# The small operations of a norm move from SBUF into the PSUM bank of its sums

## The chip, the cores and the metric

The kernel runs on one core of a Trainium2 chip. The metric is the device time of one execution in microseconds (us): before the change 1384.69, the median of three runs (1383.99 to 1385.03). A core has five engines with their own instruction queues: TensorE (PE in the profile; its weight loads are PEld), VectorE (DVE), ScalarE (ACT), GpSimd (POOL) and SyncE (SP), from whose queue most DMAs are issued. SBUF and PSUM are its memories; TensorE writes PSUM, in 8 banks of 512 fp32 numbers per partition.

## What is computed

Two layers of a decoder, on 1024 tokens of width 1024 in fp32. Each layer normalises its input, modulates it with vectors made from c, projects it, runs two kinds of attention (layer 0: latent and windowed; layer 1: differential and forgetting), gates the result, projects it back, normalises again and adds it to x. Every norm has this form:

```python
def rmsnorm(x, g):
    xf = x.astype(jnp.float32)
    y = xf * lax.rsqrt(jnp.mean(xf * xf, axis=-1, keepdims=True) + NORM_EPS)
    return (y * g.astype(jnp.float32)).astype(x.dtype)

for layer in range(DEPTH):
    mod = cond @ w_ada[layer] + b_ada[layer]
    shift, scale, gate = jnp.split(mod, 3, axis=-1)
    h = rmsnorm(x, g_pre[layer]) * (1.0 + scale[:, None, :]) + shift[:, None, :]
    y = even_mixer(h, ...) if layer % 2 == 0 else odd_mixer(h, ...)
    x = x + gate[:, None, :] * rmsnorm(y, g_post[layer])
```

The latent attention also normalises its two low-rank inputs, and the differential attention each head's output.

## The kernel before

Tiles are 128 channels by 512 tokens (C = 512), so the tokens form two halves, ch or c 0 and 1. An fp32 product is made of three matmuls: weights and activations are split into a high and a low part (split, L89 to L92: ScalarE writes the high part, VectorE or GpSimd the low one), and kstep (L124) issues high by high (L127), high by low (L128) and low by high (L130). A projection accumulates 8 such steps in a PSUM bank named pj, S or o. PSUM is given out by tag: S one tile of two banks, pt two banks, pj two, o two.

**The norm.** Channels lie on partitions, so the mean over channels is a sum over partitions, and TensorE makes it. rstd (L197) takes the squares s, summed over channel tiles, and multiplies them with a column of ones (L204): four matmuls leave the sum of each token in a pt bank, 128 tokens by 4 columns. VectorE turns it into the inverse root by eleven operations on 128x4 numbers. L206 makes the variance v from the bank; L207 makes a first guess y from v's bits; then three Newton rounds: w = -0.5 v y (L209), w = w y (L210), y = (w + 1.5) y (L212). v, w and y are small SBUF tiles of the tag sm, which has 24 buffers. Then TensorE broadcasts y over the partitions into another pt bank (L216): each column of y, stretched to 128x128, times the identity, so four matmuls. The bank r is what rstd returns, and the caller multiplies by it. Each fp32 matmul shows in the profile as two rows, so the four are x8 there.

rstd runs 21 times: twice for the input of layer 0 (run), four times for the low-rank inputs (keep, in even_first; two of them write the last y into the constant rkc), twice for the input of layer 1 (to_odd), five times for the outputs of the layers (residual), and 8 times for the heads of the differential attention (diff_items).

**What sets the order.** Each engine works through its queue in order. A scheduler in the framework builds the queues from the program, by its own estimate of what each instruction costs, and adds the waits. The program itself interleaves: project() with the norms around it, weave() with attention and projections, and ada_behind() spreads the product of c with w_ada through the projections: VectorE accumulates loaded tiles of in_wadab into the tile ad (L282), ScalarE starts each sum (L285).

Other lines that the steps touch: the softmax of a block is L463 on VectorE (row minimum from S) and L465 on ScalarE (exp with row sums); L941 and L942 in diff_items make the factor of the second map from these sums, L944 combines the two maps; L474 and L475 make reciprocal row sums for a layout change; L356 is the gate; L673 the low part of a low-rank input; L678 its squares added on GpSimd; L549 and L553 finish a head; L687 the rotation of the shared key; L246 casts a mask.

Of the kernel before, what the change touches and what calls it, by code (L numbers as in the profile page):

```python
# [33 lines left out]
class Trunk:  # L34
# [162 lines left out]
    def rstd(self, s, n, col=None):  # L197


        nc = self.nc  # L200
        nb = s.shape[-1] // 128
        p = self.psum("pt")
        for b in range(nb):
            nc.tensor.matmul(p[:, b:b + 1], s[:, b * 128:b * 128 + 128], self.ones, start=True, stop=True)  # L204
        v, w, y = (self.small(nb) for _ in range(3))
        nc.vector.tensor_scalar(v, p[:, :nb], 1.0 / n, EPS, op0=ALU.mult, op1=ALU.add)  # L206
        nc.vector.tensor_scalar(y.bitcast(I32), v.bitcast(I32), -0.5, 1597463007.0, op0=ALU.mult, op1=ALU.add)  # L207
        for i in range(3):
            nc.vector.scalar_tensor_tensor(out=w, in0=v, scalar=-0.5, in1=y, op0=ALU.mult, op1=ALU.mult)  # L209
            nc.vector.tensor_tensor(out=w, in0=w, in1=y, op=ALU.mult)  # L210
            z = col if i == 2 and col is not None else y
            nc.vector.scalar_tensor_tensor(out=z, in0=w, scalar=1.5, in1=y, op0=ALU.add, op1=ALU.mult)  # L212
        y = z
        r = self.psum("pt")[:, :nb * 128]
        for b in range(nb):
            nc.tensor.matmul(r[:, b * 128:b * 128 + 128], y[:, b:b + 1].to_broadcast([128, 128]), self.ident,  # L216
                             start=True, stop=True)
        return r
# [1218 lines left out]
```

## Time and profile before

| | us |
|---|---|
| median of 3 runs | 1384.69 |
| the profiled execution | 1385.66 |
| its span in the trace | 1383.9 |
| PE busy | 1281.1 (93%) |
| DVE busy | 918.0 (66%) |
| ACT busy | 731.9 (53%) |
| POOL busy | 334.2 (24%) |

The 1.8 us between the profiled execution and its span lie outside the trace. A row of the timeline gives start and length in us, engine, line, operation, the tile written and the tiles read (buffer numbers left out), their shapes, and in brackets how long the engine had stood idle before and what it waited for. A row of waits gives who waited for whom: us in total, times, and the longest. A group of a line gives busy us and the mean ns of one, then the idle time before; the rows of one source line give the shortest, median and longest ns. In a table of stretches each row has start and end, their length, the busy us of PE, PEld, DVE, ACT and POOL with their counts, the clock that TensorE was granted (1.00 is full speed), the DMA share and GB/s.

### The profile page before, as it was taken

The numbers are of one execution on the slowest core, as the hardware profiler recorded it, in microseconds if no ns is written. First come the engines' busy times: TensorE is split into PE (matmuls) and PEld (weight loads), VectorE is DVE, ScalarE is ACT, GpSimd is POOL, SyncE is SP. The second block draws the span as 40 slices with busy tenths as digits, with TensorE's granted clock in tenths as the row PEclk, the third lists the DMA queues.
The fourth block names the chain that finished last, engine by engine and source line by source line (L and its number), as shares of the span: only waits on it lengthen the run. The fifth ranks groups of instructions, "written<-read, shape, count | busy, mean of one in ns | idle before, by whom it ended". The sixth has DMA issues, their size and how long they took to land.

```text
span 1383.9 us, 20791 instructions
## 1 busy us (share of the span) xinstructions
PE 1281.1 (93%) x6940; PEld 1060.0 (77%) x6940; DVE 918.0 (66%) x1963; ACT 731.9 (53%) x1507; POOL 334.2 (24%) x316
## 2 busy tenths in 40 slices
PE   2798999999999999899989999999999999999996
PEld 2577788888777777777767778787888888888896
DVE  6855666777668775787977785767645464655375
ACT  4252126665557577764545544446445454556552
POOL 2242422331233215300013232221212111112400
PEclk9899999999999999999999999999999999999998
DMA  8605586556354544373633222212112121233283
GB/s 291 236 19 168 169 286 221 164 168 178 97 172 132 158 132 131 108 232 110 193 89 94 75 70 68 57 49 88 58 46 75 49 85 54 84 107 107 77 262 127
DMA packets 105132, 175.98 MB, mean 127 GB/s; under 512 B 16688, under 2 KB 25904, under 8 KB 105024
## 3 DMA queue, kind: packets, MB, share of 16 engines
q1 hardware_dynamic: 100512, 172.03, 39.4%
q10 hardware_dynamic: 4512, 2.62, 0.6%
q8 instruction: 54, 0.88, 0.3%
q14 instruction: 54, 0.44, 0.1%
HBM read 131.45 MB, written 31.74 MB: 118 GB/s over the span
## 4 chain that ended last, share of the span: by engine, by line
PE 59%; DVE 21%; issue 7%; ACT 6%; DMA 5%; POOL 1%; SPq 1%; DVEq 0%; POOLq 0%; ACTq 0%
PE pj L127 10%; PE pj L128 10%; PE pj L130 9%; PE S L441 7%; PE pt L500 4%; PE o L510 2%; DVE p L463 2%; PE S L127 2%; PE S L130 2%; PE o L509 2%; PE S L128 2%; DVE pt_l L92 2%; PE pt L216 1%; DVE acc L282 1%; DMA wr<-in_wout_dram 1%
## 5 line engine op out<-in xcount | busy, mean ns | idle before, releaser
L127 PE MATMUL pj<-h,wh 128*128 128x512 f32 (+1 forms) x816 | 340.6, 418 | 1.0 <-ACT wh L91 1.0
L128 PE MATMUL pj<-h,wh 128*128 128x512 f32 (+1 forms) x816 | 321.6, 394 | 0.0
L130 PE MATMUL pj<-h,wl 128*128 128x512 f32 (+1 forms) x800 | 314.9, 394 | 2.7 <-DVE wl L92 2.7
L92 POOL TENSOR_TENSOR wl<-wr,wh 128x512 fp32r<-128x512 f32 x126 | 164.2, 1311 | 462.7 <-ACT wh L91 424.4
L465 ACT ACTIVATE p<-p,sm 128x128 f32<-128x128 f32 (+3 forms) x192 | 148.7, 775 | 148.0 <-DVE sm L463 143.5
L92 DVE TENSOR_TENSOR pt_l<-pt,pt_h 128x512 fp32r<-128x512 f32 (+1 forms) x232 | 147.1, 635 | 107.4 <-ACT pt_h L91 105.7
L441 PE MATMUL S<-qk,qk 96*128 96x512 f32 (+5 forms) x720 | 174.6, 344 | 20.4 <-DVE sm L463 10.9
L91 ACT ACTIVATE pt_h<-pt 128x512 fp32r<-128x512 f32 (+1 forms) x232 | 127.8, 552 | 96.1 <-PE pt L500 92.5
L130 PEld LDWEIGHTS pj<-h,wl 128*128 128x128 f32 x800 | 150.5, 188 | 34.5 <-DVE wl L92 3.6
L441 PEld LDWEIGHTS S<-qk,qk 128*128 128x128 f32 (+1 forms) x720 | 120.8, 189 | 62.6 <-DVE sm L463 26.2
L127 PEld LDWEIGHTS pj<-h,wh 128*128 128x128 f32 (+1 forms) x816 | 153.6, 188 | 19.0 <-ACT wh L91 1.9
L128 PEld LDWEIGHTS pj<-h,wh 128*128 128x128 f32 (+1 forms) x816 | 154.1, 189 | 16.3 <-DVE h L92 0.2
L91 ACT ACTIVATE wh<-wr 128x512 fp32r<-128x512 f32 x165 | 101.2, 622 | 111.2 <-PE S L128 40.8
L500 PE MATMUL pt<-ident,p 128*128 128x128 f32 x840 | 134.4, 274 | 2.6 <-DVE p L944 2.6
L500 PEld LDWEIGHTS pt<-ident,p 128*128 128x128 f32 x840 | 101.2, 140 | 25.6 <-DVE p L944 4.1
L463 DVE CUSTOM_DVE_ANT_0 p<-S,mask 128x640 f32<-128x640 f32 (+7 forms) x128 | 95.9, 749 | 32.7 <-PE S L441 32.1
L509 PE MATMUL o<-pt_h,v 128*128 128x256 f32 (+1 forms) x408 | 106.5, 281 | 1.3 <-ACT pt_h L91 0.8
L510 PE MATMUL o<-pt_l,v 128*128 128x256 f32 (+1 forms) x408 | 102.3, 285 | 4.9 <-DVE pt_l L92 4.7
L347 POOL TENSOR_TENSOR t<-t,rs 128x512 f32<-128x512 f32 x26 | 36.8, 1417 | 230.8 <-DMA t<-t 208.3
L510 PEld LDWEIGHTS o<-pt_l,v 128*128 128x128 f32 x408 | 77.2, 189 | 14.8 <-DVE pt_l L92 9.6
L509 PEld LDWEIGHTS o<-pt_h,v 128*128 128x128 f32 x408 | 77.1, 189 | 9.5 <-ACT pt_h L91 3.4
L463 DVE CUSTOM_DVE_ANT_0 p<-S,x 128x128 f32<-128x128 f32 (+3 forms) x64 | 48.2, 753 | 25.0 <-PE S L445 21.8
(315 smaller groups left out, 2311.3 us busy)
## 6 DMA issues: line engine op xcount, KB each, us to landing
wr<-in_wod_dram SPq DMA_DIRECT2D x80, 256.0 KB
wr<-in_wout_dram SPq DMA_DIRECT2D x68, 256.0 KB
ad<-in_wadab_dram SPq DMA_DIRECT2D x41, 256.0 KB
wr<-in_wev_dram SPq DMA_DIRECT2D x38, 256.0 KB
raw<-in_wadaa_dram SPq DMA_DIRECT2D x32, 256.0 KB
ogd<-t SPq DMA_DIRECT2D x32, 256.0 KB
t<-t SPq DMA_DIRECT2D x106, 64.0 KB
t<-rd SPq DMA_DIRECT2D x48, 128.0 KB
```

What stands on the lines that cost most here:

```text
L91: nc.scalar.activation(hi, src, AF.Copy)
L92: (lo_eng or nc.vector).tensor_tensor(out=lo, in0=src, in1=hi.bitcast(F32), op=ALU.subtract)
L127: nc.tensor.matmul(p, w[0][:, k, :m], h[0], start=first, stop=False)
L128: nc.tensor.matmul(p, w[0][:, k, :m], h[1], start=False, stop=last and w[1] is None)
L130: nc.tensor.matmul(p, w[1][:, k, :m], h[0], start=False, stop=last)
L347: nc.gpsimd.tensor_tensor(out=s, in0=s, in1=self.rs[:, cs], op=ALU.mult)
L441: nc.tensor.matmul(dst, a, k[:, s], start=(n == 0), stop=(n == len(q) - 1 and not more))
L463: nc.vector.tensor_tensor_reduce(out=P[:, :n], in0=S[:, :n], in1=add, scale=-scale, scalar=init, op0=ALU.add, op1=ALU.min, accum_out=nm)
L465: nc.scalar.activation(P[:, :n], P[:, :n], AF.Exp, bias=nm, scale=-1.0, accum_out=l)
L500: nc.tensor.transpose(pt[:, n * 128:n * 128 + 128], b, self.ident)
L509: nc.tensor.matmul(o[:, qcols], w, hi[:, cols], start=start, stop=False)
L510: nc.tensor.matmul(o[:, qcols], w, lo[:, cols], start=False, stop=stop)
```

## The change

```diff
     def rstd(self, s, n, col=None):
 
 
+
         nc = self.nc
         nb = s.shape[-1] // 128
         p = self.psum("pt")
         for b in range(nb):
             nc.tensor.matmul(p[:, b:b + 1], s[:, b * 128:b * 128 + 128], self.ones, start=True, stop=True)
-        v, w, y = (self.small(nb) for _ in range(3))
+        v, w, y = p[:, 8:8 + nb], p[:, 16:16 + nb], self.small(nb)
         nc.vector.tensor_scalar(v, p[:, :nb], 1.0 / n, EPS, op0=ALU.mult, op1=ALU.add)
```

v and w become columns 8 and 16 on of p, the pt bank that holds the sums. y stays in SBUF. So L206 goes from PSUM to PSUM, L207 from PSUM to SBUF, L209 and L210 read one operand in PSUM and y in SBUF and write PSUM, L212 reads w in PSUM and y in SBUF and writes SBUF. Before, all but L206 had all operands in SBUF. Each norm takes one sm buffer instead of three, and p stays in use until the last L212. The counts of instructions stay: 231 of these small operations. A blank line moves all lines from 200 on up by one, so L206 of before is L207 of after.

The scheduler also orders the queues differently. Three places:

**TensorE at the third norm** (the first low-rank input of the first half; S_969 and S_957 are the bank of a projection that runs meanwhile, pt_828 and pt_822 the broadcast of this norm, pt_835 and pt_829 the sums of the next). Before:

```order
L127 MATMUL S_969<-h_316,wh_944 128x512
L128 MATMUL S_969<-h_317,wh_944 128x512
L130 MATMUL S_969<-h_316,wl_945 128x512
L216 MATMUL pt_828<-ident,sm_816 128x128 x4
L204 MATMUL pt_835<-ones,t_641 128x1 x4
L127 MATMUL S_969<-h_396,wh_944 128x512
```

After, from the same matmul on:

```order
L127 MATMUL S_957<-h_314,wh_932 128x512
L128 MATMUL S_957<-h_315,wh_932 128x512
L130 MATMUL S_957<-h_314,wl_933 128x512
L127 MATMUL S_957<-h_394,wh_932 128x512
L128 MATMUL S_957<-h_395,wh_932 128x512
L130 MATMUL S_957<-h_394,wl_933 128x512
L127 MATMUL S_957<-h_399,wh_932 128x512
L217 MATMUL pt_822<-ident,sm_810 128x128 x4
L205 MATMUL pt_829<-ones,t_637 128x1 x4
L128 MATMUL S_957<-h_400,wh_932 128x512
```

The broadcast moved behind four more matmuls of the projection; between it and its own sums stand 16 matmuls, where 12 stood.

**VectorE at the same norm**, from the second small operation on (sm_814, sm_815, sm_816 are v, w, y before; pt_805 holds v and w after). Before:

```order
L207 TENSOR_SCALAR sm_816<-sm_814 128x4
L209 SCALAR_TENSOR_TENSOR sm_815<-sm_814,sm_816 128x4
L210 TENSOR_TENSOR sm_815<-sm_815,sm_816 128x4
L212 SCALAR_TENSOR_TENSOR sm_816<-sm_815,sm_816 128x4
L209 SCALAR_TENSOR_TENSOR sm_815<-sm_814,sm_816 128x4
L210 TENSOR_TENSOR sm_815<-sm_815,sm_816 128x4
L673 SCALAR_TENSOR_TENSOR qk_803<-pj_777,vecs,qk_802 128x512
L212 SCALAR_TENSOR_TENSOR sm_816<-sm_815,sm_816 128x4
L209 SCALAR_TENSOR_TENSOR sm_815<-sm_814,sm_816 128x4
L210 TENSOR_TENSOR sm_815<-sm_815,sm_816 128x4
L212 SCALAR_TENSOR_TENSOR sm_816<-sm_815,sm_816 128x4
L246 CAST mask<-t_913 128x128
```

After:

```order
L208 TENSOR_SCALAR sm_810<-pt_805 128x4
L210 SCALAR_TENSOR_TENSOR pt_805<-pt_805,sm_810 128x4
L211 TENSOR_TENSOR pt_805<-pt_805,sm_810 128x4
L213 SCALAR_TENSOR_TENSOR sm_810<-pt_805,sm_810 128x4
L674 SCALAR_TENSOR_TENSOR qk_799<-pj_773,vecs,qk_798 128x512
L210 SCALAR_TENSOR_TENSOR pt_805<-pt_805,sm_810 128x4
L211 TENSOR_TENSOR pt_805<-pt_805,sm_810 128x4
L213 SCALAR_TENSOR_TENSOR sm_810<-pt_805,sm_810 128x4
L210 SCALAR_TENSOR_TENSOR pt_805<-pt_805,sm_810 128x4
L211 TENSOR_TENSOR pt_805<-pt_805,sm_810 128x4
L247 CAST mask<-t_901 128x128
L213 SCALAR_TENSOR_TENSOR sm_810<-pt_805,sm_810 128x4
```

The low part of the low-rank input (L673) stands one round earlier, and the cast of the mask moved ahead of the norm's last operation.

**VectorE at the end of the first head norm of the differential attention** (sm_7923 and sm_7901 are its y; the reciprocal works on the row sums of the softmax block that runs meanwhile). Before:

```order
L209 SCALAR_TENSOR_TENSOR sm_7922<-sm_7921,sm_7923 128x4
L210 TENSOR_TENSOR sm_7922<-sm_7922,sm_7923 128x4
L212 SCALAR_TENSOR_TENSOR sm_7923<-sm_7922,sm_7923 128x4
L941 RECIPROCAL sm_7964<-sm_7964 128x1
L942 SCALAR_TENSOR_TENSOR sm_7964<-sm_7964,nlam,sm_7691 128x1
```

After:

```order
L210 SCALAR_TENSOR_TENSOR pt_7896<-pt_7896,sm_7901 128x4
L942 RECIPROCAL sm_7942<-sm_7942 128x1
L211 TENSOR_TENSOR pt_7896<-pt_7896,sm_7901 128x4
L943 SCALAR_TENSOR_TENSOR sm_7942<-sm_7942,nlam,sm_7671 128x1
L213 SCALAR_TENSOR_TENSOR sm_7901<-pt_7896,sm_7901 128x4
```

The last two operations of the norm moved behind the reciprocal. On SyncE's queue, in the same part of the program as the third to sixth norm, two loads of in_wl moved ahead of loads of in_wadab.

## The prediction

> **What bounds the kernel now.** I read the page first, then PE's waits, then the timeline around the longest of them.
>
> ```profile
> span 1383.9 us, 20791 instructions
> PE 1281.1 (93%) x6940; PEld 1060.0 (77%) x6940; DVE 918.0 (66%) x1963; ACT 731.9 (53%) x1507; POOL 334.2 (24%) x316
> PE 59%; DVE 21%; issue 7%; ACT 6%; DMA 5%; POOL 1%; SPq 1%; DVEq 0%; POOLq 0%; ACTq 0%
> ```
>
> TensorE (PE) is busy for 93% and carries most of the chain that ended last. VectorE (DVE) carries a fifth of it. So the small operations matter only where PE stands still for them, and PE's waits for the broadcast (L216) say how much that is:
>
> ```profile
> PE pt L216 <- DVE sm L212: 9.7, 6, 3.4
> PE pt L216 <- issue: 2.3, 1, 2.3
> PE pt L216 <- DVE rkc L212: 1.1, 1, 1.1
> ```
>
> That is 13.1 us over 8 of the 21 norms. The last norm shows what the chain of eleven small operations costs with nothing else in the way (start, length, both in us):
>
> ```profile
> 1372.81 0.16 DVE L206 TENSOR_SCALAR sm<-pt 128x2 f32<-128x2 f32 x1 [0.76 <-PE pt L204]
> ...
> 1374.77 0.16 DVE L212 SCALAR_TENSOR_TENSOR sm<-sm,sm 128x2 f32<-128x2 f32 x1
> 1375.08 0.68 PE L216 MATMUL pt<-ident,sm 128*128 128x128 f32 x4 [2.31 <-DVE sm L212]
> ```
>
> Ten steps take 1374.77 - 1372.81 = 1.96 us, 0.196 each, and PE resumes 2.27 us after L206 started. The first norm's 2.3 us ("issue") is of the same kind. The longest wait is not:
>
> ```profile
> 111.03 1.30 POOL L678 TENSOR_TENSOR t<-t,t 128x512 f32<-128x512 f32 x1 [5.20 <-ACT t L671]
> 111.27 1.08 DVE L207 TENSOR_SCALAR sm<-sm 128x4 int32<-128x4 int32 x1
> 112.28 3.20 POOL L92 TENSOR_TENSOR p<-wr,p 128x512 fp32r<-128x512 f32 x3
> 112.38 1.21 DVE L209 SCALAR_TENSOR_TENSOR sm<-sm,sm 128x4 f32<-128x4 f32 x1
> 113.62 1.19 DVE L210 TENSOR_TENSOR sm<-sm,sm 128x4 f32<-128x4 f32 x1
> 114.85 0.65 DVE L212 SCALAR_TENSOR_TENSOR sm<-sm,sm 128x4 f32<-128x4 f32 x1
> 115.81 0.75 DVE L673 SCALAR_TENSOR_TENSOR qk<-pj,vecs,qk 128x512 fp32r<-128x512 f32 x1
> 117.36 2.05 PE L216 MATMUL pt<-ident,sm 128*128 128x128 f32 x8 [3.43 <-DVE sm L212]
> ```
>
> Four operations on four numbers per partition take 1.08, 1.21, 1.19 and 0.65 us. L207 ends at 112.35, as GpSimd's (POOL) 111.03 instruction ends at 112.33; L212 ends at 115.50, as POOL's three end at 115.48. They are held while POOL runs, and go on when it changes instruction or stops. Which instructions are held?
>
> ```profile
> L206 DVE TENSOR_SCALAR sm<-pt x21: 150/161/163, 22.0 to 1372.8; 128x4 f32<-128x4 f32 x19, 128x2 f32<-128x2 f32 x2
> L209 DVE SCALAR_TENSOR_TENSOR sm<-sm,sm x63: 143/162/1205, 22.4 to 1374.4; 128x4 f32<-128x4 f32 x57, 128x2 f32<-128x2 f32 x6
> L549 DVE TENSOR_TENSOR t<-o,t x48: 641/689/696, 232.4 to 1314.6; 64x512 f32<-64x512 f32 x48
> L553 DVE TENSOR_TENSOR t<-t,g x24: 679/684/1749, 266.0 to 1316.0; 128x512 f32<-128x512 f32 x24
> ```
>
> The numbers are shortest, median and longest in ns. L553, with both inputs in SBUF, is stretched to 1749 ns; L549, one of whose inputs is the PSUM tile o, never passes 696 in 48. L206 reads PSUM alone and stays at 163, while L209 goes to 1205. An operation that takes an input from PSUM was not held; L207, held above, takes its only input from SBUF.
>
> **The change part by part.** *The operands.* All eleven operations of a norm now take their first tensor input from the bank. So the holding should end for them. What it costs in all:
>
> ```profile
> L207 DVE TENSOR_SCALAR sm<-sm 128x4 int32<-128x4 int32 (+1 forms) x21 | 5.4, 258 | 0.5
> L209 DVE SCALAR_TENSOR_TENSOR sm<-sm,sm 128x4 f32<-128x4 f32 (+1 forms) x63 | 11.2, 177 | 1.7
> L210 DVE TENSOR_TENSOR sm<-sm,sm 128x4 f32<-128x4 f32 (+1 forms) x63 | 13.5, 214 | 1.6
> L212 DVE SCALAR_TENSOR_TENSOR sm<-sm,sm 128x4 f32<-128x4 f32 (+1 forms) x61 | 12.6, 207 | 1.8
> ```
>
> 42.7 us for 208 instructions; at 0.16 each it would be 33.3, so 9.4 us of VectorE's time is holding. Only what reaches PE counts.
>
> *The duration.* L206 reads PSUM in 161 ns, L209 reads SBUF in 162, so reading costs nothing. No VectorE row writes PSUM, so I bound that: not below -0.02 us per operation (L209's shortest against its median), not above +0.16 (the operation doubled). I take 0, because the nearest row, L206, shows no price for PSUM on its reading side. [...]
>
> *The order.* The scheduler places the broadcast later on PE, as the first rows shown with the change tell of the norm that made PE wait at 117.36. Four matmuls moved ahead of the broadcast: 16 stand between it and its sums, where 12 stood. A matmul of this form takes 0.23 us, start to start:
>
> ```profile
> 130.99 0.40 PE L127 MATMUL S<-h,wh 128*128 128x512 f32 x1
> 131.22 0.40 PE L128 MATMUL S<-h,wh 128*128 128x512 f32 x1
> ```
>
> Elsewhere the same happens, by 2 to 10 matmuls or scores, except in the first and last norm and in that of the second to_odd, where the distance stays. On VectorE (the second rows shown with the change) one cast came in ahead of the norm's last operation. Unheld, the chain is 2.27 us, plus 0.55 for L674 (before's L673: 0.75 long, in place of a 0.2 step) and 0.2 for the cast: about 3.0 us, from 111.1 to 114.1. PE ran dry at 117.36 - 3.43 = 113.93; with four matmuls more it reaches the broadcast at 114.86. The wait goes entirely. What is late next there is PE itself.
>
> *The clock.* A wait of that length costs twice (stretch, length, PE busy and count, then the other engines, then granted clock):
>
> ```profile
> 117.40:123.80 6.40, 6.40 (x23) 5.82 (x24) 3.28 (x15) 0.80 (x2) 0.00 (x0) 0.50 0.13 41
> 123.80:129.00 5.20, 5.20 (x25) 4.21 (x25) 3.93 (x11) 0.60 (x1) 0.00 (x0) 1.00 0.82 269
> 810.10:813.10 3.00, 2.99 (x12) 2.79 (x13) 1.73 (x4) 0.90 (x2) 0.04 (x1) 0.50 0.00 0
> ```
>
> For 6.4 us behind the wait the granted clock is 0.50: 3.2 us lost. Behind the wait at 810.11 it is 0.50 for 3.0 us: 1.5 lost. The three other waits that can go, with what held the chain at two of them:
>
> ```profile
> 135.45 1.15 DVE L210 TENSOR_TENSOR sm<-sm,sm 128x4 f32<-128x4 f32 x1
> 138.13 1.13 PE L216 MATMUL pt<-ident,rkc 128*128 128x128 f32 x8 [1.15 <-DVE rkc L212]
> 776.44 0.82 PE L216 MATMUL pt<-ident,sm 128*128 128x128 f32 x5 [1.15 <-DVE sm L212]
> 806.08 1.22 DVE L212 SCALAR_TENSOR_TENSOR sm<-sm,sm 128x4 f32<-128x4 f32 x1
> 808.13 1.11 DVE L210 TENSOR_TENSOR sm<-sm,sm 128x4 f32<-128x4 f32 x1
> 810.11 2.08 PE L216 MATMUL pt<-ident,sm 128*128 128x128 f32 x8 [2.25 <-DVE sm L212]
> ```
>
> At 138.13, 1.0 us of holding goes and six matmuls (1.4 us) more stand ahead: 1.15 gained. At 810.11 the rows at 806.08 and 808.13 alone hold 1.06 and 0.95 us: 2.0 of the 2.25 from these, the rest from the matmul and the two scores that now stand ahead; 2.25 gained. At 776.44 a new wait comes. As the third rows shown with the change tell, the norm's last two operations now stand behind the reciprocal of the next softmax block (L941, now L942):
>
> ```profile
> DVE sm L941 <- ACT p L465: 14.8, 20, 1.4
> ```
>
> The reciprocal waits for row sums from ScalarE (14.8 / 20, 0.7 us a time), and behind it wait the two operations, the broadcast on PE and all that PE has behind that. I count 0.2 of the 1.15 as gained there. Elsewhere the reciprocal of L474 comes in the same way; the 2 to 10 matmuls ahead of the broadcast cover it.
>
> *The bank.* p is held until the chain's end, not until L206. The next use of that bank stands behind the broadcast on PE in all 21 norms, so it costs nothing; without that cover it would cost a chain, 2 us. Two of 24 buffers fewer per norm cost nothing: no wait is for them.
>
> *The sum.* 3.4 + 3.2 + 1.15 + 0.2 + 2.25 + 1.5 = 11.7 us. Not all of it arrives. Just behind the first three terms VectorE waits for loads of in_wadab, whose pace PE does not set:
>
> ```profile
>   DVE ad L282: 8.3, 8
> 161.10 0.50 PE L127 MATMUL S<-qk,p 128*128 128x512 f32 x1 [1.66 <-DVE t L356]
> ```
>
> and on SyncE's queue two loads of in_wl now stand ahead of in_wadab's. I take a quarter off, by choice: 8.8 us. The profiled execution took 1385.66 us (span 1383.9 and 1.8 around it), so 1376.9; the median of the runs is 0.97 lower, so **1376.0**, a gain of 0.6%. Own range: 1369 (nothing lost, and some of the other held operations counting too) to 1380.5.
>
> **The rivals.** *The gain is taken back* between 140 and 175 us and where VectorE is the later engine (the 21% of the chain): L282's waits grow by what PE gains. Then 2 us or less are left: 1382.7 to 1384.7. For it: 161.10 above. Against it: in most places the wait before PE was VectorE's holding.
>
> *PSUM costs more.* There are 21 x 11 = 231 operations, and 19 of the norms have, by my estimate from the matmuls ahead, 0.5 us of cover. A price of p per operation costs 231p - 9.5 us. At p = 0.07, the middle of the bounds above, that is 6.7, which leaves 2.1 and a time of 1382.6. [...]
>
> **The slower rival** is the same mechanism beyond the point where it decides, 8.8 = 231p - 9.5, p = 0.08: a write to PSUM that the next operation reads comes back late. At 0.10 it is 13.6 us, so 1389.5. For it: no row writes PSUM from VectorE. Against it: L206.
>
> *The holding stays*, because it sits on something other than inputs from SBUF, the write say. Then only the later broadcast helps, 0.9 us at 117.36, 1.15 at 138.13 and half a microsecond at 810, 2.5 in all: about 1382.2. Against it: 48 L549 that were never held.
>
> **How the numbers follow.** A difference under 0.2% (2.8 us) can't be told from none here. Forecast 0.65; taken back 0.10; PSUM dearer by 0.04 to 0.08, 0.09, half of it faster, half the same; the slower rival 0.09; holding stays 0.07, a third of it faster. That makes faster 0.65 + 0.05 + 0.02 = 0.72, same 0.18 and slower 0.10, in which 0.01 is for a taken-back gain that comes out below nothing. The range 1369 to 1385 leaves out the slower rival and some chance below.
>
> **What would show it.** Right: L208 to L213 have no row over 0.25 us; PE's waits for the broadcast shrink to the first and last norm (4.6 us) and little else; the granted clock is 1.00 around 117 and 810. Wrong: steps of the chain well over 0.2 us in the last norm; rows over 1 us under POOL's; or the waits of PE moved to L282, L356 or L465 in the same stretches.

## The result and the profile after

The changed kernel takes **1375.16 us** (median of 6 runs, 1372.87 to 1378.71), the kernel before 1384.34 beside it (6 runs, 1383.21 to 1388.72): a ratio of 0.9925, 95% interval 0.9908 to 0.9941. In a second series it was 1376.38 against 1385.20, ratio 0.9936, 0.9919 to 0.9953. The profiled execution took 1375.71 us, its span is 10.0 us shorter than before's.

The page of the changed kernel first, span and busy times:

```profile
span 1373.9 us, 20797 instructions
PE 1274.9 (93%) x6940; PEld 1056.0 (77%) x6940; DVE 905.0 (66%) x1963; ACT 732.0 (53%) x1507; POOL 333.4 (24%) x316
```

PE is busy for 6.2 us less, though it does the same 6940 matmuls: that part of the gain is clock, as the mean granted clock also says (0.984 over the profiled execution before, 0.989 now). The other 3.8 us are waits. These are PE's waits for the broadcast, and three others that grew:

```profile
PE pt L217 <- DVE sm L213: 2.9, 3, 2.3
PE pt L217 <- issue: 2.3, 1, 2.3
PE S L442 <- DVE sm L464: 12.4, 19, 2.4
PE S L130 <- DVE wl L92: 5.1, 1, 5.1
PE S L128 <- DVE h L333: 2.9, 1, 2.9
```

The last three before the change:

```profile
PE S L441 <- DVE sm L463: 10.9, 17, 1.5
PE S L130 <- DVE wl L92: 4.1, 1, 4.1
PE S L128 <- DVE h L332: 1.3, 1, 1.3
```

The waits for the broadcast fell from 13.1 to 5.2 us. The wait for the softmax's row minimum (L464, before L463) rose from 10.9 to 12.4, that for a weight's low part (L130) from 4.1 to 5.1, that on L333 (L332 before) from 1.3 to 2.9. So of 7.9 us that left the broadcast about half came back under other names.

The small operations themselves, one source line each (shortest, median and longest in ns):

```profile
L207 DVE TENSOR_SCALAR pt<-pt x21: 155/170/171, 22.9 to 1361.8; 128x4 f32<-128x4 f32 x19, 128x2 f32<-128x2 f32 x2
L208 DVE TENSOR_SCALAR sm<-pt x21: 148/161/163, 23.1 to 1362.0; 128x4 int32<-128x4 int32 x19, 128x2 int32<-128x2 int32 x2
L210 DVE SCALAR_TENSOR_TENSOR pt<-pt,sm x63: 150/170/171, 23.3 to 1363.4; 128x4 f32<-128x4 f32 x57, 128x2 f32<-128x2 f32 x6
L211 DVE TENSOR_TENSOR pt<-pt,sm x63: 145/170/171, 23.5 to 1363.6; 128x4 f32<-128x4 f32 x57, 128x2 f32<-128x2 f32 x6
L213 DVE SCALAR_TENSOR_TENSOR sm<-pt,sm x61: 131/161/163, 23.7 to 1363.8; 128x4 f32<-128x4 f32 x55, 128x2 f32<-128x2 f32 x6
```

No row passes 0.2 us any more; the means of L209, L210 and L212, 177, 214 and 207 ns before, are now 167, 167 and 159. An operation that writes the bank has a median of 170 ns, one that writes SBUF 161: the write costs 9 ns, the read nothing. Nor does a result that was written to the bank come back late to the next operation: in the last norm, where nothing is in the way, the ten steps take 1363.76 - 1361.76 = 2.00 us, where they took 1.96.

The third norm, where PE waited 3.43 us:

```profile
110.86 1.30 POOL L679 TENSOR_TENSOR t<-t,t 128x512 f32<-128x512 f32 x1 [5.20 <-ACT t L672]
110.91 0.17 DVE L207 TENSOR_SCALAR pt<-pt 128x4 f32<-128x4 f32 x1 [4.34 <-PE pt L205]
112.11 3.33 POOL L92 TENSOR_TENSOR p<-wr,p 128x512 fp32r<-128x512 f32 x3
113.47 0.15 DVE L213 SCALAR_TENSOR_TENSOR sm<-pt,sm 128x4 f32<-128x4 f32 x1
114.50 1.05 PE L217 MATMUL pt<-ident,sm 128*128 128x128 f32 x8
```

GpSimd (POOL) runs the same four instructions beside the chain, and the eleven operations take 113.62 - 110.91 = 2.71 us from the start of the first to the end of the last, where before they took from 111.08 to 117.21, 6.13 us. The broadcast has no bracket: PE did not wait.

### The profile page after: what moved, and what is told of

Read it like the earlier page. It is cut to its first block, busy times and chain, and to the rows that moved or that the text cites. A ratio compares the mean times of both kernels' runs of the same rounds, so it can differ in the third digit from the quotient of the medians.

```text
span 1373.9 us, 20797 instructions
## 1 busy us (share of the span) xinstructions
PE 1274.9 (93%) x6940; PEld 1056.0 (77%) x6940; DVE 905.0 (66%) x1963; ACT 732.0 (53%) x1507; POOL 333.4 (24%) x316
## 4 chain that ended last, share of the span: by engine, by line
PE 54%; DVE 19%; DMA 9%; issue 8%; ACT 7%; SPq 2%; POOL 1%; DVEq 0%; POOLq 0%; ACTq 0%
PE pj L127 9%; PE pj L128 9%; PE pj L130 9%; PE S L442 7%; PE pt L501 4%; PE o L511 2%; DMA wr<-in_wout_dram 2%; DVE p L464 2%; PE S L127 2%; PE o L510 2%; PE S L130 2%; PE S L128 2%; DVE pt_l L92 2%; ACT p L466 1%; DVE t L347 1%
## 5 line engine op out<-in xcount | busy, mean ns | idle before, releaser
L130 PE MATMUL pj<-h,wl 128*128 128x512 f32 (+1 forms) x800 | 315.9, 395 | 1.6 <-DVE wl L92 1.6
L92 POOL TENSOR_TENSOR wl<-wr,wh 128x512 fp32r<-128x512 f32 x126 | 165.4, 1322 | 473.6 <-ACT wh L91 429.0
L92 DVE TENSOR_TENSOR pt_l<-pt,pt_h 128x512 fp32r<-128x512 f32 (+1 forms) x232 | 147.0, 635 | 107.7 <-ACT pt_h L91 106.0
L442 PE MATMUL S<-qk,qk 96*128 96x512 f32 (+5 forms) x720 | 174.7, 344 | 21.5 <-DVE sm L464 12.4
L130 PEld LDWEIGHTS pj<-h,wl 128*128 128x128 f32 x800 | 151.0, 189 | 34.0 <-DVE wl L92 3.1
L464 DVE CUSTOM_DVE_ANT_0 p<-S,mask 128x640 f32<-128x640 f32 (+7 forms) x128 | 96.0, 750 | 33.8 <-PE S L442 33.0
L348 POOL TENSOR_TENSOR t<-t,rs 128x512 f32<-128x512 f32 x26 | 36.5, 1402 | 238.5 <-DMA t<-t 159.6
L464 DVE CUSTOM_DVE_ANT_0 p<-S,x 128x128 f32<-128x128 f32 (+3 forms) x64 | 48.2, 753 | 25.2 <-PE S L446 21.9
```

Source lines behind the costliest of these rows:

```text
L92: (lo_eng or nc.vector).tensor_tensor(out=lo, in0=src, in1=hi.bitcast(F32), op=ALU.subtract)
L130: nc.tensor.matmul(p, w[1][:, k, :m], h[0], start=False, stop=last)
L348: nc.gpsimd.tensor_tensor(out=s, in0=s, in1=self.rs[:, cs], op=ALU.mult)
L442: nc.tensor.matmul(dst, a, k[:, s], start=(n == 0), stop=(n == len(q) - 1 and not more))
L464: nc.vector.tensor_tensor_reduce(out=P[:, :n], in0=S[:, :n], in1=add, scale=-scale, scalar=init, op0=ALU.add, op1=ALU.min, accum_out=nm)
```

## The experiments

**The order alone, the operands alone.** Every engine's queue is pinned to a given order, by edges between neighbours that order the issue and wait for nothing. One kernel has the SBUF operands of before in the order of after, the other the PSUM operands of after in the order of before. (In the kernel with SBUF operands and the order of after, v and w have a tag of their own with two buffers of 8 columns, and sm has 22 instead of 24.) In the traces, each of the two has its operations on all four computing engines in the sequence that it was given. No run has the pinning alone, without another change.

```diff
+        for a, b in zip(L, L[1:]):      # L: one engine's instructions in the wanted order
+            tc.add_manual_dep(b, a.name, info, reason="order")
...
-        v, w, y = (self.small(nb) for _ in range(3))
+        vw, y = self.t("vw", [128, 8]), self.small(nb)
+        v, w = vw[:, :nb], vw[:, 4:4 + nb]
```

Expected of the order alone:

> SBUF operands as before, but every engine's queue in the order that after has. Theory (holding by GpSimd ends): the small operations are held as before, about 42 us for the 208 (rows over 1 us remain), PE's waits for the broadcast fall only by what the later broadcast covers, from 13.1 to 9 to 11 us, the clock stays at 0.50 for some us behind the longest of them, and the time is 1380 to 1383. Rival (the order does it): PE's waits for the broadcast fall to about 5 us and the time is 1374 to 1377, though the rows over 1 us stay.

Measured: 1386.27 us, ratio 0.9996 (0.9982 to 1.0010). Expected of the operands alone:

> Variance and half product in PSUM as after, but every engine's queue in the order that before has. Theory (holding ends): no small operation over 0.25 us, the wait at 117 nearly gone with the order of before too (unheld, the chain ends within 0.3 us of the moment at which PE ran dry), PE's waits for the broadcast 5 to 6.5 us, time 1374.5 to 1378. Rival (the order does it): small operations short, but the waits at 117 and 810 keep 1 us or more each, and the time is 1380 to 1383.

Measured: 1377.18 us, ratio 0.9937 (0.9919 to 0.9956). The waits of PE with the order alone (first rows), then with the operands alone:

```profile
PE S L442 <- DVE sm L464: 13.2, 20, 1.9
PE pt L217 <- DVE sm L213: 6.2, 6, 2.6
...
PE pt L217 <- issue: 3.2, 1, 3.2
...
PE pt L217 <- DVE rkc L213: 1.0, 1, 1.0
```

```profile
PE S L442 <- DVE sm L464: 12.3, 19, 1.6
PE pt L217 <- DVE sm L213: 4.1, 5, 2.3
...
PE pt L217 <- issue: 2.3, 1, 2.3
...
PE pt L217 <- DVE rkc L213: 0.4, 2, 0.2
```

With the operands alone the waits for the broadcast are 6.8 us by these rows, a little over the 5 to 6.5 expected, and the broadcast of the third norm, at 115.63, has no wait. The operands carry the gain; neither series of the whole change stands apart from them alone. The rival (the order does it) fell. But the theory missed on the order too: the waits for the broadcast fell to 10.4 us (6.2, 3.2, and 1.0 for rkc), as it said, and the time did not fall to the 1380 to 1383 expected. At the second head norm, where before PE waited 2.25 us, one can see why. The kernel with the order alone there, DVE, POOL and PE:

```profile
806.06 2.55 POOL L92 TENSOR_TENSOR wl<-wr,wh 128x512 fp32r<-128x512 f32 x2 [4.51 <-ACT wh L91]
807.41 1.21 DVE L213 SCALAR_TENSOR_TENSOR sm<-vw,sm 128x4 f32<-128x4 f32 x1
809.05 1.25 DVE L213 SCALAR_TENSOR_TENSOR sm<-vw,sm 128x4 f32<-128x4 f32 x1
810.42 0.82 DVE L464 CUSTOM_DVE_ANT_0 p<-S,mask 128x640 f32<-128x640 f32 x1
811.30 0.50 PE L442 MATMUL S<-qk,qk 128*128 128x512 f32 x1 [1.87 <-DVE sm L464]
812.02 1.91 PE L217 MATMUL pt<-ident,sm 128*128 128x128 f32 x8
```

The broadcast waits no longer, because two scores stand ahead of it; but these wait for the row minimum L464, which stands on VectorE behind the held operations. Moving an instruction behind others covers a wait only if those others do not wait for the same engine; here the first of them waited 1.87 us for it.

**One operand at a time.** Both in the order of after, with v or w alone in the bank:

```diff
-        v, w = vw[:, :nb], vw[:, 4:4 + nb]
+        v, w = p[:, 8:8 + nb], vw[:, 4:4 + nb]      # the one
+        v, w = vw[:, :nb], p[:, 16:16 + nb]         # the other
```

> Only the variance in PSUM, the half product and y in SBUF, order of after. Theory (an operation whose inputs all lie in SBUF is held): L208 and L210 (first input from PSUM) have no row over 0.25 us, L211 and L213 (both inputs in SBUF) keep rows over 1 us; what L208 and L210 no longer lose is partly lost by the operation behind them, which runs into the same GpSimd instruction, so 30 to 60 in 100 of the holding goes; time 1377 to 1381. Rival (holding sits on the write to SBUF): L208, L210, L211 and L213 all keep rows over 1 us, and the time is that of the order alone.

> Only the half product in PSUM, the variance and y in SBUF, order of after. Theory (inputs decide): L208 and L210 (inputs in SBUF; L210 writes PSUM) keep rows over 1 us, L211 and L213 (one input from PSUM) have none over 0.25 us; time 1376.5 to 1381. Rival (holding sits on the write): L210 and L211, which write PSUM, have no row over 0.25 us, L208 and L213, which write SBUF, keep them.

Measured: 1380.34 us, 0.9967 (0.9956 to 0.9978), and 1381.99 us, 0.9972 (0.9959 to 0.9984), the second just above the 1376.5 to 1381 expected. The lines with v alone in the bank, then with w alone:

```profile
L210 DVE SCALAR_TENSOR_TENSOR vw<-pt,sm x63: 131/161/163, 23.0 to 1368.9; 128x4 f32<-128x4 f32 x57, 128x2 f32<-128x2 f32 x6
L213 DVE SCALAR_TENSOR_TENSOR sm<-vw,sm x61: 134/161/1274, 23.4 to 1369.3; 128x4 f32<-128x4 f32 x55, 128x2 f32<-128x2 f32 x6
```

```profile
L210 DVE SCALAR_TENSOR_TENSOR pt<-vw,sm x63: 152/170/1221, 23.2 to 1370.8; 128x4 f32<-128x4 f32 x57, 128x2 f32<-128x2 f32 x6
L213 DVE SCALAR_TENSOR_TENSOR sm<-pt,sm x61: 131/161/164, 23.6 to 1371.2; 128x4 f32<-128x4 f32 x55, 128x2 f32<-128x2 f32 x6
```

L210 with both inputs in SBUF is held although it writes PSUM (1221), and L210 with one input from PSUM is not although it writes SBUF (163): the holding sits on the inputs, and the rival fell. In the time each half brings 0.3% of the whole's 0.6 to 0.75%. In VectorE's time it is less: the 208 operations of L208 to L213 take 45.6 us with the order alone, 42.8 with v, 41.9 with w and 34.0 with both in the bank, so 24 and 32 in 100 of the holding went, below the 30 to 60 that I gave for v. The operation behind the one set free runs into the same GpSimd instruction: at the third norm with v alone, L208 and L210 take 0.16 us each, and then L211 0.67 and L213 1.21 us beside the GpSimd instructions that held L208 and L210 before.

**The forms by themselves.** VectorE runs eleven forms with GpSimd idle and beside GpSimd (a and b in SBUF, f and g in PSUM; the lines for tensor_scalar and scalar_tensor_tensor are of the same kind):

```python
for _ in range(k):
    v.tensor_tensor(out=c, in0=a, in1=b, op=ALU.mult)   # L18; out=f is L20
for _ in range(k):
    v.tensor_tensor(out=c, in0=f, in1=b, op=ALU.mult)   # L22; out=g is L24
...
for k in range(240):
    nc.gpsimd.tensor_tensor(out=z, in0=u[:, :C], in1=u[:, C:], op=ALU.mult)
```

> Nothing of the kernel's computation: VectorE runs 16 operations of each of eleven forms on 128x4 numbers while GpSimd is idle, then the same while GpSimd runs 240 products of 128x512 from SBUF, then 4 of each on 128x512. Theory (inputs decide): with GpSimd idle every form takes 0.13 to 0.18 us; beside GpSimd the forms with all tensor inputs in SBUF (whether they write SBUF or PSUM) go to 1 us or more, those with an input from PSUM stay under 0.2 us, whether they write PSUM or SBUF. Rival (the write decides): the forms that write PSUM stay short even with both inputs in SBUF. Rival (PSUM is dearer): forms that read PSUM take 0.06 us more than those that read SBUF with GpSimd idle.

The groups with GpSimd idle (busy us, mean ns; p is PSUM, s is SBUF):

```profile
L20 DVE TENSOR_TENSOR p<-s 128x4 f32<-128x4 f32 x16 | 2.7, 170 | 0.5
L18 DVE TENSOR_TENSOR s<-s 128x4 f32<-128x4 f32 x16 | 2.6, 162 | 6.1 <-DMA s<-in_x_dram 5.6
L22 DVE TENSOR_TENSOR s<-p,s 128x4 f32<-128x4 f32 x16 | 2.6, 161 | 0.6
```

The same beside GpSimd, with the forms of one input (L32, L34), and two of 128x512:

```profile
L20 DVE TENSOR_TENSOR p<-s 128x4 f32<-128x4 f32 x16 | 10.4, 649 | 0.5
L18 DVE TENSOR_TENSOR s<-s 128x4 f32<-128x4 f32 x16 | 10.2, 637 | 0.6
L32 DVE TENSOR_SCALAR s<-s 128x4 f32<-128x4 f32 x16 | 9.8, 612 | 0.6
L18 DVE TENSOR_TENSOR s<-s 128x512 f32<-128x512 f32 x4 | 5.6, 1395 | 0.1
L34 DVE TENSOR_SCALAR p<-s 128x4 f32<-128x4 f32 x16 | 2.6, 166 | 0.5
L22 DVE TENSOR_TENSOR s<-p,s 128x4 f32<-128x4 f32 x16 | 2.6, 161 | 0.6
L22 DVE TENSOR_TENSOR s<-p,s 128x512 f32<-128x512 f32 x4 | 2.8, 691 | 0.1
```

Two inputs in SBUF are held whatever is written, at 128x512 too (1395 ns against 691), though on 128x4 their mean is 0.59 to 0.65 us and not the 1 us or more expected; an operation with an input from PSUM never is (161 to 169 ns on 128x4, 691 to 697 at 128x512); and the price of PSUM is some 9 ns on the write (170 against 161 and 162) and none on the read. Only tensor_scalar from SBUF pays no such price: with GpSimd idle it takes 170 ns into SBUF and 166 into PSUM. One form answers against the theory: L34, tensor_scalar from SBUF into PSUM, was not held (166 ns), though its only input lies in SBUF, while L32 into SBUF was. So for an operation with one input the destination counts too: beside GpSimd, from SBUF, 612 ns into SBUF and 166 into PSUM. Why it does, no row shows. The rival with a dearer PSUM fell here too: with GpSimd idle a read of PSUM costs not 0.06 us more, but nothing (161 ns for L22 with one input in PSUM, 162 for L18 with both in SBUF).

**What is late next.** In the changed kernel PE waits at 808.50, in the place of the wait at 810.11. First the changed kernel, then one in which the product of a head with its gate is VectorE's:

```diff
-                        nc.gpsimd.tensor_tensor(out=z, in0=z, in1=st["g"][c], op=ALU.mult)
+                        nc.vector.tensor_tensor(out=z, in0=z, in1=st["g"][c], op=ALU.mult)
```

> The changed kernel once more, beside the next two on the same chip. Theory (the operands carry the gain, the later broadcast next to nothing): 0.6 to 0.9% under before, so that it does not stand apart from the run with the operands alone by more than 0.2%.

> The change, and the product of a head with its gate (L969, 8 times 1.29 us) taken from GpSimd to VectorE. Theory (the holding that is left hits the next operations with both inputs in SBUF): the two operations of L399 behind the second head norm, 2.48 us together beside it, fall to 1.4 us there and PE's wait of 2.40 us at 808.50 shrinks by 0.5 us or more; but VectorE gets 8 operations of 0.69 us more, so the time stays within 2 us of the change's. Rival (that wait has another cause): it stays at 2.2 us or more, and the time grows by 1 to 4 us.

```profile
804.09 1.29 POOL L969 TENSOR_TENSOR t<-t,g 128x512 f32<-128x512 f32 x1 [1.46 <-DVE t L968]
804.18 2.48 DVE L399 TENSOR_TENSOR qk<-t,qk 64x512 fp32r<-64x512 f32 x2
808.50 0.50 PE L442 MATMUL S<-qk,qk 128*128 128x512 f32 x1 [2.40 <-DVE sm L464]
```

```profile
803.60 0.69 DVE L969 TENSOR_TENSOR t<-t,g 128x512 f32<-128x512 f32 x1
804.32 1.40 DVE L399 TENSOR_TENSOR qk<-t,qk 64x512 fp32r<-64x512 f32 x2
807.57 0.50 PE L442 MATMUL S<-qk,qk 128*128 128x512 f32 x1 [1.06 <-DVE sm L464]
```

The pair of L399 takes 1.40 us and the wait falls from 2.40 (1.96 in the profiled execution of the second series) to 1.06, as the theory said: the next operations with both inputs in SBUF had been held. The time is 1372.38 us, ratio 0.9904 (0.9882 to 0.9925), against 1376.38, 0.9936 (0.9919 to 0.9953, within the 0.6 to 0.9% expected), for the change beside it: 4.0 us less, more than the 2 that I allowed, though the two intervals just touch. To give GpSimd less to do seems to have paid, though VectorE got eight operations more. In this kernel and in the three that follow nothing is pinned: the scheduler ordered their queues anew, so their times hold the new order as well, and what the operands did is read from the rows.

**One more operand from PSUM.** On top of the change, the rotation's first product reads the projection's bank:

```diff
-        nc.vector.tensor_tensor(out=z, in0=z, in1=self.rc[:, cs], op=ALU.mult)
+        y = self.tmp()
+        nc.vector.tensor_tensor(out=y, in0=p, in1=self.rc[:, cs], op=ALU.mult)
...
```

> The change, and one more operation of VectorE fed from PSUM: the rotation's first product (L347, 26 times 128x512, 908 ns on average) reads the projection's bank itself instead of its copy in SBUF, and writes a tile of its own. Theory (inputs decide): its rows fall to 0.69 us, none over 0.75, which frees 5.7 us of VectorE; what PE gets of it is what stands behind it on VectorE in front of a softmax block, 0 to 3 us: 1372 to 1376. Rival (the bank): the projection's bank is held until VectorE comes to it, the next projection waits for a bank, and the time is 1377 or more.

The rows of 21 of the 26 (L347 is now L348; the other five read the tile S in 684 to 692 ns), and who waited for them:

```profile
L348 DVE TENSOR_TENSOR t<-pj,rc x21: 651/685/693, 237.3 to 888.6; 128x512 f32<-128x512 f32 x21
...
  PE S L127: 7.8, 1
```

No row is over 0.70 us, VectorE's busy time 6.0 us less than in the change beside it, and 1369.38 us: ratio 0.9886 (0.9866 to 0.9906), better than the 1372 to 1376 expected. PE's waits for the row minimum are 7.3 us, 12.0 in the change beside it. The rival's mechanism is there as well: one matmul waited 7.8 us for a bank that L348 still had to read.

**Both together**, and both with the old rotation in the dense projections at the start of layer 1, where that wait stood:

> The change with both edits of the last two runs: the rotation's first product from the projection's bank, and the product of a head with its gate on VectorE. Theory (each takes holding away at places of its own): the gains over the change, 0.5% and 0.3%, add up: 0.983 to 0.988 of before, 1364 to 1369. Rival (they take away the same waits): no more than the rotation alone, 0.9875 to 0.990.

> As the run before, but in the dense projections at the start of layer 1, whose banks are given out five in turn, the rotation's first product goes back to the copy in SBUF; in all others it reads the bank. Theory (there the bank is held too long: a matmul waited 7.80 us for L348 at 691.84 with the rotation from the bank alone): that wait goes, part of it comes back as the waits of the change for weights (5.08 us for L92 at 704.26), and the time is 0 to 4 us under the run before: 0.9835 to 0.9866 of before. Rival (those waits are the same time under another name): no difference, 0.9856 to 0.9876.

Measured: 1366.71 us, 0.9866 (0.9849 to 0.9884), the lowest median of all and in the range expected if the gains add up; but the interval overlaps that of the rotation alone, so that they add up is not shown. The other took 1370.33 us, 0.9893 (0.9870 to 0.9916). It did not help, where 0 to 4 us less were expected: the wait for L348 (6.7 us in the run before) went and 5.2 us for a weight (L92) came back, as in the change. Whether it is slower than the one before is open, since the intervals overlap.

## Why the prediction was right

- **What is held, and that it ends.** Right for all eleven operations, by their rows above and by the two half changes. That L207 of before was held for its input alone was too wide: its destination in SBUF was needed too, by L32 and L34 of the forms (612 ns into SBUF, 166 into PSUM).
- **The write at nothing.** 147 of the 231 write the bank; at 9 ns that is 1.3 us of VectorE's time, most of it under cover. The two rivals with a dearer PSUM fell: no run shows the 0.04 to 0.08 us per operation, or more, that their chances stood for; the rows gave 9 ns on a write and nothing on a read.
- **117.36, 3.4 us, and the clock behind it, 3.2.** Both came. The chain took 2.71 us to its last end, some 2.9 to PE by the 0.15 that the last norm of before needs from there, where 3.0 were reckoned; and behind it the clock, 0.50 for 6.4 us before, is full (stretch, length, busy times, granted clock):

```profile
114.50:120.90 6.40, 5.88 (x35) 4.81 (x33) 5.23 (x17) 1.29 (x3) 0.94 (x2) 1.00 0.84 281
```

- **138.13, 1.15 us.** It came: the broadcast there, at 134.01, has no wait.
- **776.44, 0.2 us.** Too small, the whole 1.15 went. With the operands alone 1.14 us stayed there, though nothing of the norm was held: in between stood two operations with inputs from SBUF (L423) that took 2.39 us. In the change the same two took 1.40: GpSimd's instruction started 0.72 us behind their start, not 0.52, so just behind the start of the second, and it was GpSimd's that became long (1.84 us instead of 1.32). That term hung on where GpSimd stood, not on the reciprocal.
- **810.11, 2.25 us.** The step that failed. The chain there was shortened as reckoned, but what is late next was not PE: it was VectorE, on whose queue L399 behind the norm was held, for 1.08 us, and PE waited 2.40 us for the row minimum instead. With the operands alone the wait came back too, as 1.58 us at 807.85, there behind two other operations with inputs from SBUF (L347, 1.50 us, and L943, 1.23). Only the clock behind it, 1.5 us, came (first row):

```profile
808.50:812.00 3.50, 3.50 (x20) 3.01 (x21) 1.31 (x4) 2.41 (x5) 1.29 (x1) 1.00 0.09 22
1364.07:1370.00 5.93, 1.19 (x4) 0.89 (x4) 4.14 (x12) 0.00 (x0) 3.27 (x4) 0.50 0.27 91
```

- **The order.** This failed too. I gave the later broadcast a part in three terms, and 2.5 us if it stood alone. Alone it was worth nothing (0.9996).
- **A quarter off.** The sum was 11.7 us, the profiled span shows 10.0 and the medians 9.2, so the deduction was near in size, but by luck. Its reason did not show. The waits of VectorE for loads of in_wadab are 10.8 us after 8.3 (8.6 in the second series), yet between 140 and 175 us PE has no wait for L357 (before's L356, 1.66 us at 161.10), and nothing was taken back between 140 and 175 us. The lead of the change shows it, counted by matmuls done: the first 601 took 180.00 us before and 170.95 after, so PE is 9.1 us ahead there, more than the 7.75 of the first three terms. At 3450 matmuls (740.00 and 733.44) it is 6.6, at 3839 (820.00 and 811.18) 8.8, at 4863 (1020.00 and 1008.61) 11.4. So 2.5 us were lost where the prediction expected nothing, 2.6 won behind the last of its terms, and the two about cancel. What caused either was not tried. At the end the last norm lost 0.5 us, in this execution: its broadcast fell into half clock (1.19 us long, second row above; 0.68 before and in the second series).

## What to carry to other kernels

Look for VectorE operations that are far longer in some executions than in others while GpSimd runs: if both tensor inputs lie in SBUF, leave one in the PSUM bank it came from, where it can stay. Here that ended it (637 ns beside GpSimd with both in SBUF, 161 with one from PSUM), for 9 ns a write (170 against 161). Before a wait is counted as won, look on the slow engine for the next operation of the same kind ahead of what the waiting engine needs next: here 2.25 us came back as 1.58 to 2.40 under another line. And an order that moves an instruction behind others gains nothing if these wait for the same engine: here, alone, it had a ratio of 0.9996.

## What the hardware showed that was not expected

The clock does not follow the length of a wait alone. A wait of 1.87 us with the order alone (811.30) was followed by half clock (0.50), one of 2.40 in the change (808.50) by full clock (1.00 from 808.50 to 812.00). The row for the first:

```profile
812.00:815.00 3.00, 3.00 (x13) 2.80 (x12) 1.99 (x6) 1.52 (x4) 0.20 (x1) 0.50 0.01 3
```

What told the two waits apart, these rows don't show. So the cause stays open. The 3.2 and 1.5 us of clock in the sum were read from one execution, and some of the spread of the runs may be of this kind: of the change's six, the fastest (1372.87) has a mean clock of 0.992, the slowest (1378.71) 0.988. That the clock alone makes the spread was not tried.
